# Middle stage of a one-layer streaming encoder: all four engines in program order, attention units as chains, probabilities scaled on VectorE

## The chip, the cores and the metric

One core of one Trainium2 chip runs the kernel. The metric is device microseconds (us) of one execution. TensorE (PE), VectorE (DVE), ScalarE (ACT), GpSimd (POOL) and SyncE (SP, which here issues all DMAs) each take their own instructions in the order of their own queue and wait on semaphores for each other.

## The reference, cut to what matters

```python
def residual_block(x, c, mixer, ...):                 # 512 prompt tokens and 64 sample tokens, D_MODEL = 1024
    sh1, sc1, g1, sh2, sc2, g2 = split(silu(c) @ w_ada + b_ada, 6)
    h = rms_norm(x, norm1_g) * (1 + sc1) + sh1
    mix = mixer(h)                                    # 512 attention columns | 512 convolution columns
    x = x + g1 * (mix @ w_out)
    h = rms_norm(x, norm2_g) * (1 + sc2) + sh2
    return x + g2 * (square(relu(h @ w_ff1)) @ w_ff2)

def mixer(h):
    q, k, v, qi, ki, wi, ga, gb = split(h @ w_in)     # 8 heads x 64; 8 indexer heads x 64
    u = ga * sigmoid(gb)
    sc = einsum(relu(qi . ki / 8), wi * 8 ** -0.5)    # indexer score of every key
    idx = top_k(where(admissible, sc, NEG_INF), k)    # k = 128 (prompt) or 256 (sample, 1088 keys)
    p = softmax(q . k[idx] / 8 - slope * |pos - idx|)
    y = silu(layer_norm(causal depthwise conv(u, 31 taps)))
    return concat(p @ v[idx], y)
```

## The kernel before, in words

Every wide product is an fp32 product in three passes (`mm3`, L288: high by high, high by low, low by high), with tokens along the free dimension in two halves of 288. There are three stages: a start (norm, modulation, first three products), the middle (L488 to L1178), and the second half of the output projection with the MLP. In the start and in the MLP the order of PE, ACT, DVE (in the MLP also POOL) is the order of the program text; in the middle only PE's is (`tc.manual_schedule`, L1153). There a scheduler at compile time orders ACT, DVE and POOL by its own model; `tc.issue_after` ties a few of their instructions to a place.

PE's order in the middle is made by ticks. The main line is 22 column tiles of 128 (`mtile`, L357: 4 `qi`, then three pairs `gb`, `ga`, then `v`, `k`, `q` for four head pairs p), 16 `mm3` each, and then the half of the output projection that reads the convolution (`out_half(mixC)`, L1176), 64 `mm3`. After each `mm3` comes `tick()` (L344). It advances Python generators in the list `side`; each yields the number of ticks to its next step, and what it emits then stands in PE's queue between two `mm3`. `until(cond)` (L353) ticks without any `mm3` between: such ticks take no PE time of their own, and the side steps in them follow each other directly. There are four such loops: in `qkv(0)` until two convolutions are done (L845), in `qkv(p)` for p = 2, 3 until the attention of head pair p - 2 is done, at L1173 until the convolution's norm is done, and at L1177 until no side generator is left.

The side generators: `keys` (indexer keys), `scores` (indexer scores), `topk_prompt` (128 of up to 512 keys, by rounds of max and match-replace on DVE), `topk_sample` (a search over thresholds in 16 iterations: DVE sets candidates, L745, ACT counts with three Sign passes, L747, DVE decides, L748 to L751), `convs` (31 DVE taps for each of channel tiles 0 and 3), `convs_pe` (channel tiles 1 and 2 on PE, L510), `conv_norm`, `attn_prompt` (for each head pair 8 units of logits, softmax, transposition, values), `attn_sample`, `tokens` (k and v written out), `mod_rest` (16 steps of the adaptive modulation; each loads 1 MB of `w_ada` into the two buffers that its predecessor's matmuls have read) and `residual_in`. `P` (L38) holds their waits in ticks; the change leaves `P` as it is.

PSUM banks have four tags: `acc` 3, `lg` 2, `tp` 2, `av` 1. SBUF tags that matter: `pr` 2 (probabilities), `pT` 4 (their transposes; three of them hold the scores at first). A weight tile is split on ACT (`whi`, L331) and POOL (`wlo`, L332) at the start of the column tile before the one that uses it.

Of the kernel before, what the change touches and what calls it, by code (L numbers as in the profile page):

```python
# [71 lines left out]
def step_kernel(ctx: ExitStack, tc: tile.TileContext, io):  # L72
# [153 lines left out]

    def mod_steps(g, f0, nf, operand):
# [21 lines left out]
        if g != 1:  # L249
            o = mod[:, SC1 if g == 0 else SC2, :, r]  # L250
            dve.scalar_tensor_tensor(o, o, 1.0, both((R_G1 if g == 0 else R_G2) + f0), op0=OP.add, op1=OP.mult)

# [90 lines left out]

    def tick():  # L344
# [23 lines left out]
    def evac_stack(dst, scale):  # L368
        def go(j, p, cs_):
            copy_to(act, dst[A, 0, cs_], p[A], scale)  # L370
            copy_to(act, dst[B, 1, cs_], p[B], scale)
            for o, s, hi in ((dst[B, 0, cs_], A, dst[A, 0, cs_]), (dst[A, 1, cs_], B, dst[B, 1, cs_])):
                if scale is None:
                    sub(dve, o, p[s], f(hi))
                else:
                    dve.scalar_tensor_tensor(o, p[s], scale, f(hi), op0=OP.mult, op1=OP.subtract)
# [19 lines left out]
    def front(b):  # L396
        f0, nf = BLOCKS[b]
        g = mod_steps(0, f0, nf, lambda v, kh, kk: ada[b][2 * v + kh][:, kk, :])
        next(g)
        yield  # L400
        pump(g, 1)
# [83 lines left out]
    start.close()  # L485

# [9 lines left out]
    def conv_pe(c):  # L496
# [13 lines left out]
        for h in range(3):  # L510
            t = p_av()
# [5 lines left out]
            act.activation(yc[c][:, CT * h:CT * h + CT], t[:, :CT], AF.Identity, bias=cols[:, R_CB + c:R_CB + c + 1])  # L517
            yield 2
# [22 lines left out]
    def conv_state(c):  # L541
        t = p_tp()
        for s, o in enumerate((SEQ, SEQ + HALO + SAMP)):
            pe.transpose(t[:HALO, 128 * s:128 * s + 128], u[c][:, o:o + HALO], ident)
        m = mt([128, 2, 128], FT, "cso")
        copy_to(act, m[:HALO], t[:HALO, :256].rearrange("p (s x) -> p s x", s=2))
# [34 lines left out]
    def keys():  # L581
        t = p_tp()
        for i in range(5):
            n = 128 if i < 4 else SAMP
            pe.transpose(t[:n, 72 * i:72 * i + 72], kiw[:72, 128 * i:128 * i + n], ident[:72, :72])
        copy_to(act, kiwt[:, :4, :], t[:, :288].rearrange("p (i c) -> p i c", c=72))
# [7 lines left out]
        yield P["KYW"]  # L594
        for b in range(2):
            t = p_tp()
# [5 lines left out]
            yield P["KYW"]  # L602
# [9 lines left out]
    def scores():  # L612
        qis = dt_([128, 4, 2, SAMP], FR, "qis")
# [3 lines left out]
        def prompt(h):  # L617
            for i in (1, 2, 3):
                n = NKEY[i]
                t = p_lg()  # L620
# [3 lines left out]
                r = mt([128, 512], FT, "relu")  # L624
                act.activation(r[:, :n], t[:, :n], AF.Relu)
                if h == 0:
                    dve.tensor_scalar(score[i], r[:, :n], wsc[:, i, 0:1], None, op0=OP.mult)
                else:
                    dve.scalar_tensor_tensor(score[i], r[:, :n], wsc[:, i, h:h + 1], score[i], op0=OP.mult, op1=OP.add)
                if h == 7:  # L630
                    pool.memset(score[i][0:64, n - 64:n], NEG)
                yield P["IDX"]

        def sample(p):
            r = dt_([128, KEYS], FT, "srelu")
            lhs = qis[:, p].rearrange("p s t -> p (s t)")
            for c, (a, b) in enumerate(CH):
                t = p_lg() if c < 2 else p_tp()
# [3 lines left out]
                act.activation(r[:, a:b], t[:, :b - a], AF.Relu)  # L642
                yield P["IDX"] if c < 2 else 1
            if p == 0:
                dve.tensor_scalar(sacc, r, wss[:, 0:1], None, op0=OP.mult)
            else:
                dve.scalar_tensor_tensor(sacc, r, wss[:, p:p + 1], sacc, op0=OP.mult, op1=OP.add)

        def total():
            for a, b, bank_ in ((0, 512, p_lg), (512, KH, p_tp)):  # L650
                t = bank_()
# [3 lines left out]
                copy_to(act, sful[0][:, a:b], t[:, :b - a])  # L655
                yield 2
            spawn(topk_sample(sful[0]), 1)

        for p in range(4):
# [3 lines left out]
            if p < 3:  # L663
                yield from prompt(2 * p)
            yield from sample(p)
# [8 lines left out]
    def distance(i):  # L674
        n = NKEY[i]
        d = mdp.tile([128, 512], FT, name="dist", tag="pr", bufs=2)[:, :n]
        with tc.issue_after(behind[0]):
            pool.iota(d, pattern=[[-1, n]], base=128 * i, channel_multiplier=1, allow_small_or_imprecise_dtypes=True)
        act.activation(d, d, AF.Abs)
        return d  # L680

    last = [None]

    def topk_prompt():
        def steps(*ts):
# [3 lines left out]
            for m, i in zip(m8, ts):  # L689
                last[0] = dve.match_replace(score[i], m, score[i], SENT).ins  # L690

        def penalty(i):
            n = NKEY[i]
            pen = mt([128, 512], FT, "pen")
            dve.tensor_scalar(pen[:, :n], score[i], SENT, BIG, op0=OP.not_equal, op1=OP.mult)
            last[0] = dve.tensor_tensor(dm[i], pen[:, :n], distance(i), op=OP.add).ins
            flags.add(("dm", i))

        for i in (1, 2):
# [5 lines left out]
            penalty(i)  # L705
            yield
        penalty(3)
# [7 lines left out]
    def topk_sample(sful):  # L715
# [28 lines left out]
        for i in range(len(low)):  # L744
            dve.tensor_tensor(sgi[:, 12:15], sgi[:, 8:9].to_broadcast([128, 3]), bits[:, i], op=OP.bitwise_or)  # L745
            for z in range(3):
                act.activation(eq, sful, AF.Sign, bias=cands[:, z:z + 1], scale=-1.0, accum_out=cnts[:, z:z + 1])  # L747
            swap(oths, cnts)  # L748
# [3 lines left out]
            yield P["TKS"]  # L752
# [19 lines left out]
        dve.tensor_scalar(sful, eq, 0.0, BIG, op0=OP.is_equal, op1=OP.mult)  # L772
        act.activation(cum, cum, AF.Abs)
        dve.tensor_tensor(sful, sful, cum, op=OP.add)
        for s, r in enumerate((A, B)):
# [12 lines left out]
    def qkv(p):  # L788
# [4 lines left out]
        def evac_q(j, t, cs_):  # L793
            n = HALF if j == 0 else SEQ - HALF
            r = slice(HALF * j, HALF * j + n)
            for s, (own, oth) in enumerate(((A, B), (B, A))):
                copy_to(act, qd[s][own, 0, r], t[own, :n], 0.125)
                copy_to(act, qd[s][oth, 0, r], t[own, :n], 0.125)
# [612 lines left out]
```

## Time and profile before

| | |
|---|---|
| median of 3 runs | 861.04 us (860.79 to 861.17) |
| profiled execution: time, span | 860.36 us, 858.6 us |
| busy share of the span | PE 94%, DVE 52%, ACT 48%, POOL 35% |
| mean granted TensorE clock | 0.973 |
| the middle | from about 58 to 405 us of the span |

The profile's times are us from the start of the span. A PE that waits inside a run of pipelined matmuls still counts as busy, so the idle time that the view of waits names is the surer figure. A granted clock of 1.0 is 2.4 GHz; the other level is 1.2 GHz.

### The profile page before, as it was taken

How to read it: one execution, taken by the hardware profiler on the slowest of the kernel's cores; microseconds unless marked ns; L12 is line 12 of the kernel's file. 1: busy time of each engine (PE TensorE's matmuls, PEld its weight loads, DVE VectorE, ACT ScalarE, POOL GpSimd, SP SyncE). 2: the span in 40 equal slices, each digit the busy share in tenths (PEclk: the TensorE clock that was granted, in tenths of full speed). 3: DMA queues.
4: the chain of work that ended last, by engine and by line, in shares of the span. 5: the costliest groups of instructions: out<-in, count | busy, mean ns of one | idle time of the engine just before them, and what ended most of it. 6: DMA issues, size and time to landing. Idle time of an engine off the chain costs nothing.

```text
span 858.6 us, 17186 instructions
## 1 busy us (share of the span) xinstructions
PE 808.2 (94%) x6787; PEld 753.0 (88%) x6787; DVE 449.0 (52%) x1148; ACT 412.5 (48%) x976; POOL 303.5 (35%) x337
## 2 busy tenths in 40 slices
PE   5998997989798999999999999999999999999995
PEld 3797895567777988989999999999999999999995
DVE  4569879999997444654934311343113321144142
ACT  5365554555776787754745411443224522244332
POOL 0146342222244414232424343343433343343800
PEclk8799999899999999999999999999999999999998
DMA  8984157247343343732222323223222323223312
GB/s 241 309 205 123 53 146 184 60 100 187 112 113 110 116 137 115 222 122 77 74 74 75 97 76 93 80 75 99 74 77 82 88 83 90 74 74 101 120 55 57
DMA packets 164555, 95.57 MB, mean 111 GB/s; under 512 B 7699, under 2 KB 161119, under 8 KB 164475
## 3 DMA queue, kind: packets, MB, share of 16 engines
q1 hardware_dynamic: 164475, 94.48, 39.2%
q8 instruction: 53, 0.87, 0.4%
q14 instruction: 27, 0.22, 0.1%
HBM read 88.82 MB, written 5.64 MB: 110 GB/s over the span
## 4 chain that ended last, share of the span: by engine, by line
PE 69%; DVE 17%; ACT 7%; DMA 3%; issue 3%; POOL 1%; SPq 0%; ACTq 0%; DVEq 0%; POOLq 0%
PE ps_acc L290 11%; PE ps_acc L291 11%; PE ps_acc L292 11%; PE ps_lg L292 5%; PE ps_lg L290 5%; PE ps_lg L291 5%; DVE yc L564 3%; PE ps_av L292 3%; PE ps_av L290 2%; PE ps_av L291 2%; DVE score L690 2%; DVE m L688 2%; PE ps_tp L234 2%; DMA ada<-w_ada 1%; PE ps_av L887 1%
## 5 line engine op out<-in xcount | busy, mean ns | idle before, releaser
L332 POOL TENSOR_TENSOR wlo<-wraw,whi 128x512 fp32r<-128x512 f32 x172 | 222.6, 1314 | 378.3 <-ACT whi L106 378.0
L290 PE MATMUL ps_acc<-h,whi 128*128 128x288 f32 (+1 forms) x608 | 190.8, 314 | 0.0
L291 PE MATMUL ps_acc<-h,whi 128*128 128x288 f32 (+1 forms) x608 | 181.7, 299 | 0.0
L292 PE MATMUL ps_acc<-h,wlo 128*128 128x288 f32 (+1 forms) x608 | 181.1, 298 | 0.0
L106 ACT ACTIVATE whi<-wraw 128x512 fp32r<-128x512 f32 x172 | 99.8, 621 | 126.4 <-issue 120.6
L290 PEld LDWEIGHTS ps_acc<-h,whi 128*128 128x128 f32 x608 | 116.2, 191 | 14.3 <-issue 12.4
L291 PEld LDWEIGHTS ps_acc<-h,whi 128*128 128x128 f32 x608 | 116.7, 192 | 0.8
L292 PEld LDWEIGHTS ps_acc<-h,wlo 128*128 128x128 f32 x608 | 116.3, 191 | 0.0
L1266 ACT ACTIVATE z<-z,bs 128x224 f32<-128x224 f32 (+2 forms) x96 | 40.2, 450 | 98.6 <-DVE z L1262 98.6
L1087 DVE SCALAR_TENSOR_TENSOR x<-ps_acc,mod,x 128x288 f32<-128x288 f32 (+3 forms) x91 | 36.2, 420 | 83.6 <-PE ps_acc L292 83.0
L564 DVE SCALAR_TENSOR_TENSOR yc<-u,cw,yc 128x606 f32<-128x606 f32 x60 | 58.4, 981 | 0.6
L292 PE MATMUL ps_acc<-a,wlo 128*128 128x288 f32 x192 | 56.7, 295 | 0.0
L290 PE MATMUL ps_acc<-a,whi 128*128 128x288 f32 x192 | 56.6, 295 | 0.0
L291 PE MATMUL ps_acc<-a,whi 128*128 128x288 f32 x192 | 56.6, 295 | 0.0
L292 PE MATMUL ps_lg<-h,wlo 128*128 128x288 f32 (+1 forms) x176 | 52.2, 296 | 0.8 <-POOL wlo L332 0.8
L291 PE MATMUL ps_lg<-h,whi 128*128 128x288 f32 (+1 forms) x176 | 52.2, 297 | 0.0
L290 PE MATMUL ps_lg<-h,whi 128*128 128x288 f32 (+1 forms) x176 | 52.2, 296 | 0.1
L747 ACT ACTIVATE gc<-sful,sg 128x544 bf16<-128x544 f32 x48 | 35.8, 746 | 28.6 <-DVE sg L745 27.8
L872 POOL TENSOR_SCALAR prob<-prob,mx 128x128 f32<-128x128 f32 (+3 forms) x32 | 20.2, 631 | 56.8 <-DVE mx L871 34.2
L1087 DVE SCALAR_TENSOR_TENSOR x<-ps_lg,mod,x 128x64 f32<-128x64 f32 (+4 forms) x34 | 12.7, 407 | 52.5 <-PE ps_lg L292 52.5
L292 PE MATMUL ps_lg<-a,wlo 128*128 128x288 f32 x128 | 37.8, 295 | 0.0
L290 PE MATMUL ps_lg<-a,whi 128*128 128x288 f32 x128 | 37.8, 295 | 0.0
(358 smaller groups left out, 2019.0 us busy)
## 6 DMA issues: line engine op xcount, KB each, us to landing
wraw<-w_ff SPq DMA_DIRECT2D x64, 512.0 KB
ada<-w_ada SPq DMA_DIRECT2D x44, 512.0 KB
wraw<-w_in SPq DMA_DIRECT2D x24, 512.0 KB
wraw<-w_out SPq DMA_DIRECT2D x8, 512.0 KB
rep<-ud SPq DMA_DIRECT2D x24, 115.0 KB
xtok<-x_prompt SPq DMA_DIRECT2D x4, 512.0 KB
ada<-w_ada SPq DMA_DIRECT2D x8, 256.0 KB
ct<-cache_k SPq DMA_DIRECT2D x8, 256.0 KB
```

The costliest lines, as they stand in the source:

```text
L106: act.activation(out, in_, AF.Copy, scale=1.0 if scale is None else scale)
L234: pe.matmul(t[r:r + 32, :w], lhsT=cs[:, 4 * kh + kk, :], rhs=operand(v, kh, kk), start=kk == 0, stop=kk == 3, tile_position=(0, r))
L290: pe.matmul(out, lhsT=hi, rhs=src[:, 0, cs_], start=first, stop=False)
L291: pe.matmul(out, lhsT=hi, rhs=src[:, 1, cs_], start=False, stop=False)
L292: pe.matmul(out, lhsT=lo, rhs=src[:, 0, cs_], start=False, stop=last)
L332: behind[0] = pool.tensor_tensor(lo[:, c], raw[:, c], f(hi[:, c]), op=OP.subtract).ins
L564: dve.scalar_tensor_tensor(yc[c], src, w, yc[c], op0=OP.mult, op1=OP.add)
L688: dve.max(m, score[i])
L747: act.activation(eq, sful, AF.Sign, bias=cands[:, z:z + 1], scale=-1.0, accum_out=cnts[:, z:z + 1])
L872: pool.tensor_scalar(pt[:, :n], pt[:, :n], m[:, 1:2], 1.0, op0=OP.mult, op1=OP.mult)
L1087: dve.scalar_tensor_tensor(xm[:, a:b], t[:, a - r.start:b - r.start], mod[:, g, s, m:m + 1], xm[:, a:b], op0=OP.mult, op1=OP.add)
L1266: act.activation(y, y, AF.Relu, bias=bs[:, s:s + 1])
```

## The change: what it does

It sets ACT, DVE and POOL of the middle in program order too, drops `issue_after`, and moves each step that reads another engine's result some ticks behind it: `after(n, do)` puts a closure into the list `due`, which `tick()` runs n ticks later, before the side generators. A dictionary `room` counts free buffers by tag; `yield from have(tag)` ticks until one is free, `free(tag)` returns it.

What the cut diff below leaves out: in `conv_pe`, `out` is the same activation and then `free(tag)`; in `prompt`, the relu stays in its PSUM bank and `add` frees the bank and does the same multiply-add from there (the third tile uses the `av` bank); `penalty(i)` becomes iota on POOL, 4 ticks, Abs on ACT, 3 ticks, and two DVE steps that reuse the score tile; in `evac_q` and `evac_k` all ACT copies come first, the DVE steps `after(3)` and the copies of their results `after(6)`; a unit of the attention goes on with transpositions, 2 ticks, ACT's copy, 3 ticks, and with s = 1 the values, 2 ticks, ACT, 2 ticks, DVE; `attn_sample` gets such passages too; `spread` gets 2, 2, 2 and 3 ticks between its steps; `conv_norm` uses one `lg` and one `tp` bank for the mean, waits 3 ticks in each of its four steps, 10 in place of CN2, and 2 before each of its four Silu; the last `until` waits for `side` and `due`.

```diff
+    room = dict(tp=2, lg=2, av=1, pr=2, pT=4)
+    def have(tag):
+        while not room[tag]:
+            yield
+        room[tag] -= 1
     def mod_steps(g, f0, nf, operand):
+        yield from have("tp")
         t = p_tp()
         ...
+        yield 3
         copy_to(act, m[:, :w], t[:, :w])
+        free("tp")
         yield P["MODL"]
+        yield from have("tp")
         t = p_tp()
         ...
+        yield 2
     def tick():
+        for e in list(due):
+            e[0] -= 1
+            if e[0] <= 0:
+                due.remove(e)
+                e[1]()
+    inner.enter_context(tc.manual_schedule(engines={mybir.EngineType.PE, mybir.EngineType.Activation, mybir.EngineType.DVE, mybir.EngineType.Pool}))
     def conv_pe(c):
         for h in range(3):
-            t = p_av()
+            tag = ("av", "lg", "av")[h]
+            yield from have(tag)
             ...
-            act.activation(yc[c][:, CT * h:CT * h + CT], t[:, :CT], AF.Identity, bias=cols[:, R_CB + c:R_CB + c + 1])
-            yield 2
+            after(2, out)
+            yield 3
     def scores():
         def prompt(h):
-                r = mt([128, 512], FT, "relu")
-                act.activation(r[:, :n], t[:, :n], AF.Relu)
+                after(2, lambda r=r: act.activation(r, r, AF.Relu))
+                after(4, add)
-            spawn(topk_sample(sful[0]), 1)
+            spawn(topk_sample(sful[0]), 5)
             if p < 3:
                 yield from prompt(2 * p)
+            else:
+                yield 4
             yield from sample(p)
             if p == 3:
                 yield from prompt(2 * p)
+                yield 6
                 yield from total()
-        spawn(topk_prompt(), 1)
+        spawn(topk_prompt(), 6)
     def topk_prompt():
-            penalty(i)
-            yield
-        penalty(3)
+            yield from penalty(i)
+        yield from penalty(3)
     def topk_sample(sful):
             dve.tensor_tensor(sgi[:, 12:15], sgi[:, 8:9].to_broadcast([128, 3]), bits[:, i], op=OP.bitwise_or)
+            yield 3
             ...
+            yield 8
             ...
-            yield P["TKS"]
     def qkv(p):
-        spawn(tokens(1), P["TKW"])
         until(lambda: all(("conv", c) in flags for c in PEC) and (p < 2 or p - 2 in flags))
+        spawn(tokens(1), 4)
-        flags.add(("qkv", p))
+        after(8, lambda: flags.add(("qkv", p)))
     def attn_prompt(p):
+        def unit(i, s):
+            yield from have("lg")
             ...
+            yield 2
+            dve.tensor_reduce(m[:, 0:1], t[:, :n], axis=AX.X, op=OP.max, negate=True)
+            yield 2
+            yield from have("pr")
+            free("lg")
+            act.activation(pt[:, :n], t[:, :n], AF.Exp, bias=m[:, 0:1], accum_out=m[:, 1:2])
+            yield 3
             dve.reciprocal(m[:, 1:2], m[:, 1:2])
-            pool.tensor_scalar(pt[:, :n], pt[:, :n], m[:, 1:2], 1.0, op0=OP.mult, op1=OP.mult)
+            dve.tensor_scalar(pt[:, :n], pt[:, :n], m[:, 1:2], None, op0=OP.mult)
+            yield 2
             ...
+        while left[0] < 4:
+            yield
         flags.add(p)
     def attn_sample(p):
+        yield from logits(1)
+        yield 2
+        yield from logits(2)
+        yield 4
         dve.tensor_reduce(m[:, 3:4], m[:, :3], axis=AX.X, op=OP.max, negate=True)
+        yield 2
         act.activation(pt, pt, AF.Exp, bias=m[:, 3:4], accum_out=m[:, 4:5])
+        yield 4
         dve.reciprocal(m[:, 4:5], m[:, 4:5])
-        pool.tensor_scalar(pt, pt, m[:, 4:5], 1.0, op0=OP.mult, op1=OP.mult)
+        dve.tensor_scalar(pt, pt, m[:, 4:5], None, op0=OP.mult)
         ...
```

## Rows read from the trace of the kernel before

**Rows 1.** Windows: us, then busy us (instructions) of five engines, granted clock, DMA.
```profile
58.00:123.00 65.00, 60.01 (x467) 55.38 (x469) 55.86 (x92) 34.83 (x82) 34.14 (x94) 0.97 0.44 116
123.00:196.00 73.00, 63.58 (x673) 45.77 (x669) 71.14 (x223) 37.07 (x92) 18.67 (x20) 0.94 0.48 124
196.00:257.00 61.00, 52.57 (x505) 46.12 (x498) 57.05 (x123) 41.94 (x114) 19.90 (x17) 0.93 0.51 134
257.00:271.00 14.00, 13.22 (x131) 12.27 (x129) 12.19 (x37) 8.38 (x22) 5.63 (x6) 1.00 0.44 120
271.00:405.00 134.00, 129.82 (x1221) 115.73 (x1219) 65.20 (x185) 90.34 (x232) 44.18 (x50) 0.99 0.44 132
```

**Rows 2.** Waits of PE, 58 to 405 us: total us, times, longest.
```profile
PE ps_av L514 <- ACT yc L517: 6.7, 3, 4.8
PE ps_tp L824 <- ACT kv L106: 4.1, 1, 4.1
PE ps_lg L622 <- ACT relu L625: 3.3, 2, 1.7
PE ps_tp L878 <- POOL prob L872: 3.2, 2, 2.0
PE ps_tp L241 <- ACT modrow L106: 2.3, 1, 2.3
```

**Rows 3.** Timeline of ACT, 147 to 151 us: start, us, instruction, idle before.
```profile
147.51 0.75 ACT L747 ACTIVATE gc<-sful,sg 128x544 bf16<-128x544 f32 x1 [4.00 <-DVE sg L745]
...
150.01 0.41 ACT L517 ACTIVATE yc<-ps_av,cols 128x202 f32<-128x202 f32 x1
```

**Rows 4.** Timeline of DVE: the sum of the convolutions' tiles.
```profile
255.54 0.79 DVE L1023 TENSOR_TENSOR csum<-csum,yc 128x606 f32<-128x606 f32 x1
```

**Rows 5.** Groups of DVE, 58 to 405 us: count, busy us, mean ns, idle before.
```profile
L695 DVE TENSOR_SCALAR pen<-score 128x256 f32<-128x256 f32 (+2 forms) x3 | 1.1, 354 | 0.0
L645 DVE TENSOR_SCALAR sacc<-srelu,wss 128x1088 f32<-128x1088 f32 x1 | 0.8, 787 | 0.0
```

**Rows 6.** Timeline of PE, two ticks apart, without and with a convolution's group.
```profile
131.28 0.30 PE L290 MATMUL ps_acc<-h,whi 128*128 128x288 f32 x1
...
131.67 0.30 PE L290 MATMUL ps_acc<-h,whi 128*128 128x288 f32 x1
...
141.37 0.55 PE L514 MATMUL ps_av<-rep,wd 128*32 128x202 f32 x8
...
142.44 0.55 PE L514 MATMUL ps_av<-rep,wd 128*32 128x202 f32 x8
```

**Rows 7.** Timeline of ACT: copies after `v` of pair 2 and in `q` of pair 2.
```profile
273.54 0.41 ACT L106 ACTIVATE kv<-ps_acc 128x288 f32<-128x288 f32 x1
...
298.50 0.40 ACT L106 ACTIVATE qd<-ps_acc 64x288 fp32r<-64x288 f32 x1
```

**Rows 8.** Waits of DVE, 58 to 405 us.
```profile
DVE mx L871 <- ACT prob L870: 12.7, 19, 1.6
```

**Rows 9.** Timeline of PE: first and last pieces of the end of the middle.
```profile
380.70 0.60 PE L924 MATMUL ps_tp<-ident,ct 128*128 128x128 f32 x4
...
401.69 1.08 PE L234 MATMUL ps_tp<-ada,cs 128*32 128x128 f32 x32
...
404.74 0.39 PE L241 MATMUL ps_tp<-sel,modrow 128*128 128x4 f32 x2
```

**Rows 10.** Chain of work that ended last: start, us, a load of 512 KB.
```profile
56.74 3.46 DMA wraw<-w_in
```

**Rows 11.** Timeline of ACT: table loads in the convolution's norm and after it.
```profile
299.34 1.28 ACT L1003 ACT_TABLE_LOAD   x1
...
312.26 1.28 ACT L1042 ACT_TABLE_LOAD   x1
...
318.34 1.28 ACT L870 ACT_TABLE_LOAD   x1 [0.71 <-DVE mod L248]
```

More of the change, by code (lines that the diff above doesn't have):

```diff
@@ L371, in go, with rest @@
             copy_to(act, dst[B, 1, cs_], p[B], scale)
[L372 to L376, printed above, removed]
+            def rest():
+                for o, s, hi in ((dst[B, 0, cs_], A, dst[A, 0, cs_]), (dst[A, 1, cs_], B, dst[B, 1, cs_])):
+                    if scale is None:
+                        sub(dve, o, p[s], f(hi))
+                    else:
+                        dve.scalar_tensor_tensor(o, p[s], scale, f(hi), op0=OP.mult, op1=OP.subtract)
+            after(2, rest)
         return go
@@ L541, in conv_state @@
     def conv_state(c):
+        yield from have("tp")
         t = p_tp()
@@ L581, in keys @@
     def keys():
+        yield from have("tp")
         t = p_tp()
@@ L617, in prompt @@
         def prompt(h):
+            while "wi" not in flags:
+                yield
             for i in (1, 2, 3):
                 n = NKEY[i]
-                t = p_lg()
+                tag = ("lg", "lg", "av")[i - 1]
+                yield from have(tag)
+                t = (p_lg, p_lg, p_av)[i - 1]()
                 lhs = qi[h // 2][:, h % 2, 128 * i:128 * i + 128]
@@ L637, in sample @@
             for c, (a, b) in enumerate(CH):
+                tag = "lg" if c < 2 else "tp"
+                yield from have(tag)
                 t = p_lg() if c < 2 else p_tp()
@@ L894, in attn_prompt @@
-        for x in range(len(units) + 3):
-            if 0 <= x - 2 < len(units):
-                turn(x - 2)
-            if x < len(units):
-                while units[x][0] and ("dm", units[x][0]) not in flags:
-                    yield
-                logits(x)
-            if x >= 4 and x % 2 == 0:
-                values((x - 4) // 2)
-            yield P["ATT"]
+            free("pr")
+            yield 2
+            yield from have("pT")
+            free("tp")
+            probT[i, s] = mdp.tile([128, 512], FT, name="probT", tag="pT", bufs=4)
@@ new lines, in unit @@
+            copy_to(act, probT[i, s][:, :n], t[:, :n])
+            yield 3
+            if s:
+                while (i, 0) not in probT:
+                    yield
+                yield from have("av")
+                av = p_av()
+                pts = [probT.pop((i, z)) for z in range(2)]
+                for c in range(i + 1):
+                    for z in range(2):
+                        pe.matmul(av[64 * z:64 * z + 64, :128], lhsT=vt[:, c, 64 * z:64 * z + 64],
+                                  rhs=pts[z][:, 128 * c:128 * c + 128], start=c == 0, stop=c == i, tile_position=(0, 64 * z),
+                                  skip_group_check=True)
+                r = slice(128 * i, 128 * i + 128)
+                free("pT", "pT")
+                yield 2
+                copy_to(act, mixT[p][:, 0, r], av[:, :128])
+                yield 2
+                sub(dve, mixT[p][:, 1, r], av[:, :128], f(mixT[p][:, 0, r]))
+                free("av")
+                left[0] += 1
@@ L904, in attn_prompt @@
+        for i in range(4):
+            for s in range(2):
+                while i and ("dm", i) not in flags:
+                    yield
+                spawn(unit(i, s))
+                yield P["ATT"]
+        while left[0] < 4:
+            yield
         flags.add(p)
@@ L1010, in spread @@
         pe.matmul(tb[:, :SAMP], lhsT=ones, rhs=dg[:, SEQ:TOK], start=True, stop=True)
+        yield 2
+        free("tp", "tp")
         copy_to(act, dst[:, :SEQ], ta)
         copy_to(act, dst[:, S], tb[:, :SAMP])
-        yield
+        yield 3
     mixC = []
     def conv_norm():
-        while "taps" not in flags:
+        while not ("taps" in flags and all(("conv", c) in flags for c in PEC)):
             yield
@@ L1147, in convs @@
             for _ in range(W - P["T0"] if c == 0 else W):
-                with tc.issue_after(last[0]):
-                    next(taps[c])
+                next(taps[c])
                 yield P["TAP"]
         flags.add("taps")
-    with tc.manual_schedule(engines={mybir.EngineType.PE}):
-        spawn(prepare(), P["PRW"])
-        spawn(keys(), P["KEYW"])
-        spawn(convs(), P["TAPW"])
-        spawn(convs_pe(), 8)
-        spawn(scores(), P["SCW"])
-        spawn(mod_rest(), P["MODW"])
-        for p in range(4):
-            mtile(evac_stack(qi[p], None))
-            spawn(bump(), P["QIW"])
-            if p == 0:
-                spawn(conv_state(0), P["CS0"])
-        glu(1)
-        glu(2)
-        glu(3)
-        spawn(conv_norm(), P["CNW"])
-        spawn(chain(*[attn_prompt(p) for p in range(4)]))
-        spawn(samples())
-        for p in range(4):
-            qkv(p)
-        until(lambda: "norm" in flags)
-        mix_conv()
-        spawn(residual_in())
-        out_half(mixC, lambda m, j: None)
-        until(lambda: not side)
+    spawn(prepare(), P["PRW"])
+    spawn(keys(), P["KEYW"])
+    spawn(convs(), P["TAPW"])
+    spawn(convs_pe(), 8)
+    spawn(scores(), P["SCW"])
+    spawn(mod_rest(), P["MODW"])
+    for p in range(4):
+        mtile(evac_stack(qi[p], None))
+        spawn(bump(), P["QIW"])
+        if p == 0:
+            spawn(conv_state(0), P["CS0"])
+    glu(1)
+    glu(2)
+    glu(3)
+    spawn(conv_norm(), P["CNW"])
+    spawn(chain(*[attn_prompt(p) for p in range(4)]))
+    spawn(samples())
+    for p in range(4):
+        qkv(p)
+    until(lambda: "norm" in flags)
+    mix_conv()
+    spawn(residual_in())
+    out_half(mixC, lambda m, j: None)
+    until(lambda: not side and not due)
+    inner.close()
     mid.close()
```

247 lines of the change are left out of this document (163 added, 84 removed).

## The prediction

> **What bounds the kernel now.** I read the windows first, to see which engine is full in which stretch; then the waits of PE, to see who holds it up; then the timelines around the longest waits. From 123 to 257 us DVE is busy 128.2 of 134 us, and PE idles 17.9 us there; from 271 to 405 us PE is busy 129.8 of 134 us and DVE half of it [rows 1]. So the middle has two parts: one in which DVE is full and PE waits now and then, and one in which PE alone is full. Over the whole middle PE idles 27.8 us (the windows' lengths less PE's busy times), and the granted clock is 0.93 to 0.97 in the first three windows: 65 x 0.03 + 73 x 0.06 + 61 x 0.07 + 134 x 0.01 = 12 us of full-clock time that was not granted [rows 1]. In such gaps the clock falls to the lower of its two levels. More than 12 + 27.8 us cannot be had.
>
> The waits are of one kind. Twelve lines make 27.2 us; the five shown make 19.6, and ACT ends 16.4 of these, POOL 3.2 [rows 2]. ACT is not full (31% idle at least in each window). It is held by order: its three Sign passes stand at the head of its queue and wait 4.00 us for DVE's candidates, and the copy that frees the convolution's bank stands behind them and starts at 150.01 [rows 3]; PE's longest wait, 4.8 us [rows 2], ends with it.
>
> **What program order does to the first part.** The change puts every step of the other engines where the program has it, so an evacuation stands behind the DVE work of earlier ticks and not behind that of later ones. The waits of [rows 2] go where DVE keeps up. But DVE's work does not shrink, so I ask how far PE is when DVE ends the convolution's taps; after that PE alone bounds.
>
> Ticks, counted from the first tile of the middle by the code. Before: `scores` ends at 94, rounds of top-k from 95, 16 rounds of 112 ticks and two single ticks, "prompt" at 209, 84 ticks of taps, "taps" at 293. After: four ticks and six ticks more make `scores` end at 104; the spawn waits 6 (110); 112 ticks of rounds; three penalties of 7; "prompt" at 243; "taps" at 327. In `qkv(0)` the loop without main work ran from 176 to 202; the two convolutions of PE now end near 217 (ten ticks for `scores`, one more per bank), so it runs 41 ticks and not 26. Main ticks behind "taps": 267 before, 286 after.
>
> DVE before ended that sum at 255.54 + 0.79 = 256.3 us [rows 4]. After, it starts the rounds some 2 us later, and has by tick 327 this work besides: the end of the sample's selection and pair 1's `q`, which before lay in 257 to 271 us (12.2 us busy [rows 1], of which I take 10), and the scaling of pair 0's probabilities: 8 of 0.354 us [rows 5] = 2.8. So DVE is there at 256.3 + 2 + 12.8 = 271 us. The 24 other scalings of units and the 4 of 0.787 us [rows 5] (11.6 us) fall behind 271 us, where DVE idles 68.8 of 134 us [rows 1]; they cost nothing while that holds.
>
> PE leads DVE, but no more than about one column tile: a weight's `whi` stands in ACT's queue behind copies that wait for DVE, and the tile after next needs it. I take 12 ticks. So at 271 us PE has 286 + 12 = 298 main ticks done. Before, at 273.54 us it had just ended `v` of pair 2 [rows 7], which is main tick 272 (298 less the 26 without main work). That is 26 main ticks ahead: at 131.67 - 131.28 = 0.39 us [rows 6], 10.3 us. Side work is ahead too: from 273.54 to 298.50 us (`q` of pair 2, 24 main ticks on [rows 7]) the PE took 25.0 us, 9.4 of it main ticks; of the 15.6 of side work and stalls I count half, 7.8, as done by then in the new order, since the attention of pair 1 starts 28 ticks later than before and sample 0 ten. Bounds 0 and 15.6. Gain: 18.1 us.
>
> **What it adds there.** DVE now stops where its next instruction is not ready. The nearest row: DVE's reciprocal waits for ACT's exponentials 12.7 us in 19 times, 0.67 each [rows 8]. Between ticks 110 and 327 there are some 12 iterations of the sample search, 8 units and 4 evacuations of such passages: 24 x 0.67 = 16 us at most, 0 where DVE is late anyway. DVE is the late engine there, so I take a quarter, 4 us.
>
> The convolutions' 48 groups of PE cost 1.07 us with their tick [rows 6], 0.68 over a plain one, in either order. In the longer loop of `qkv(0)` 24 groups lie alone, which DVE's rounds cover: it is full there. Without that cover the loop's 15 more ticks would cost PE 15 x 0.39 = 6 us.
>
> **The end of the middle.** Before, the last `w_ada` step came at 401.69 and the last product of the side work at 404.74 us [rows 9]: main line (tick 442), samples (450) and modulation (446 for step 16) ended together. After, a modulation step takes 27 + 5 = 32 ticks, so step 16 is at 41 + 15 x 32 = 521; a sample takes some 52 ticks in place of 40, from about 301, so the last ends near 509; the main line ends at 352 + 41 + 5 + 64 = 462 (5 for the loop of pair 3, as pair 1 ends near 366). From 462 on there is no `mm3` between the pieces: the last sample's chain, 457 to 509, is bare. Before it ran from 380.70 to 404.74, 24 us [rows 9] with 30 main ticks of 0.39 beside it, so 12 us of other work and passages. Behind it comes step 16, whose loads can start only when step 15 has read its buffers; a load of 512 KB took 3.46 us [rows 10], two take 4 to 7. I take 18 us for this end, in which PE has some 10 us of work of its own (that sample, the last units of pair 3, two steps). Cost: 8 us. Bounds: 0, if waits for buffers make the main line later and so cover it, and 24 - 10 = 14.
>
> What else moves: SP's queue has the same DMAs, two loads each per modulation step later; POOL loses 32 + 4 scalings and so frees itself for `wlo`, which nobody waited long for. After 271 us I set new waits equal to the 4.2 us that go. The sum: -18.1 + 4 + 8 = -6.1; 860.4 - 6.1 = 854.3, and the median of the runs lies 0.7 above the profiled execution: 855.
>
> **Rivals.**
>
> 1. DVE in order falls behind, and ACT with it (slower). Place: ticks 110 to 327. Price: the full 16 us of bare passages, 12 more than counted, and PE loses the lead of 12 ticks (4.7): 855 + 17 = 872. For: DVE is at 97% there, ACT's longest single cause of waiting is DVE [rows 3]. Against: a late engine seldom waits. It decides from a sum L1023 that ends after 281 us; forecast 275, this rival 288.
> 2. DVE does not bind PE: evacuations stand early enough, and all waits on ACT and POOL go (19.3 + 4.6 us of the twelve lines) with their share of the clock (10.5): 860.4 - 34.4 + 8 + 0.7 = 835. Against: DVE's 128 us of work in 134 [rows 1].
> 3. No change: ACT loads a function table in 1.28 us each time, three times in the norm before, because its Sqrt and four Silu fell between the exponentials of two head pairs [rows 11]. After, the norm comes at ticks 336 to 391 and pair 2's exponentials from 378 on, one every 4 ticks, while the Silu stand 2 ticks apart: some 8 loads, 5 more, 6.4 us on ACT. If PE waits for each: 855 + 6.4 = 861.5. Against: ACT idles 43.7 of 134 us there [rows 1].
>
> The Trainium skill, "ScalarE: Activation LUTs", section "Table sets: the hidden batching unit", says to batch calls by table set and not by function, which speaks against this interleaving; its section "What ACT_TABLE_LOAD costs" gives 1283 ns and 1380 ns of drain. The trace agrees on the load, 1.28 us [rows 11]; the drain is not to be seen in these rows. By the page's sum rival 3 would end at 855 + 5 x 2.66 = 868.
>
> **Numbers.** A difference under 0.2% (859.3 to 862.8) cannot be told from none. Forecast 855, own range 848 to 859: 0.38. Rival 2: 0.12. Rival 3: 0.15. Rival 1: 0.35. Faster 0.50, same 0.15, slower 0.35. The unknown terms span -25.9 (front with all side work, no end) to +19.7 (front 10.3, 16 and 14); a range of 841 to 877 leaves out most of rival 2 and the far end of rival 1.
>
> **What would show it.** Right: PE's waits for ACT `yc` L517 and `kv` L106 and for POOL's probabilities gone; L1023's successor ends near 275 us; PE mostly idle or sparse for some 8 us ahead of the products on `mix`; ACT table loads 8 or so in the norm. Wrong: that sum beyond 281 us, PE waits in the first part that end with `wlo` or with DVE, the last sample covered by main work, or a part of the time moving outside 58 to 405 us.

## The result, and the profile after

912.32 us median (909.70 to 913.18, 4 runs) against 861.11 (860.79 to 861.65, 4 runs): ratio 1.0589 [1.0565, 1.0613], slower by 51.2 us. The forecast was 855, range 841 to 877. The profiled execution has a span of 911.1 us at a mean granted clock of 0.948 (before 858.6 and 0.973).

Windows of the kernel after, the edges and columns of [rows 1] (TensorE's matmuls, its weight loads, VectorE, ScalarE, GpSimd):

```profile
58.00:123.00 65.00, 62.25 (x482) 57.71 (x481) 53.64 (x85) 35.58 (x82) 35.28 (x92) 1.00 0.46 122
123.00:196.00 73.00, 66.70 (x776) 50.73 (x775) 62.62 (x208) 35.92 (x89) 14.75 (x16) 0.95 0.56 139
196.00:257.00 61.00, 39.05 (x281) 35.81 (x279) 52.70 (x131) 37.59 (x99) 15.28 (x12) 0.83 0.34 93
257.00:271.00 14.00, 11.13 (x92) 9.98 (x92) 13.56 (x30) 8.69 (x21) 2.45 (x4) 0.76 0.07 19
271.00:405.00 134.00, 115.11 (x921) 101.38 (x915) 72.59 (x174) 82.27 (x199) 27.88 (x20) 0.87 0.36 105
```

Up to 196 us PE is busier than before. From 196 on it idles 22 of 61 us and the clock is at 0.83, and no other engine is full for long: DVE idles 8.3 of these 61 us and ACT 23.4. That is the sign of engines that wait for each other.

One window over the middle up to the same product, the 17th `mm3` on `mix` (411.4 us before, 463.0 after); first before, then after:

```profile
58.00:411.40 353.40, 325.60 (x3024) 281.68 (x3023) 266.93 (x676) 217.04 (x554) 125.10 (x188) 0.97 0.45 125
```

```profile
58.00:463.00 405.00, 346.31 (x3026) 301.46 (x3025) 286.59 (x713) 224.72 (x559) 103.31 (x150) 0.91 0.40 110
```

The window is 51.6 us longer: PE's idle time goes from 27.8 to 58.7 us (30.9 more), and its busy time from 325.6 to 346.3 (20.7 more) for the same matmuls, since more of them run at the clock's lower level (granted clock 0.97 before, 0.91 after). Of 5 us lost, 2 are clock.

Where it goes, by the start of the first `mm3` behind k main ticks in PE's timelines (TensorE's side work between them differs, so this is the lead of the main line alone). Before in us, the others as difference to it, a minus for ahead; e1 to e17 are experiments below:

| main tick | before | after | e3 | e1 | e14 | e17 |
|---|---|---|---|---|---|---|
| 144 | 167.5 | -17.2 | -18.8 | -6.5 | -8.6 | -16.4 |
| 160 (`v` of pair 0) | 177.4 | -13.0 | -14.6 | -2.1 | -4.4 | -12.2 |
| 180 (in `k`, behind the loop of `qkv(0)`) | 204.8 | -11.4 | -7.4 | +16.1 | +10.4 | +7.4 |
| 192 (`q` of pair 0) | 209.8 | -3.8 | -6.3 | +17.2 | +11.7 | +9.3 |
| 208 | 223.7 | -7.6 | -12.2 | +14.3 | +10.6 | +2.7 |
| 256 | 262.2 | +9.4 | +4.7 | +12.5 | +16.0 | +5.3 |
| 304 | 308.1 | +10.5 | -2.3 | +2.7 | +8.4 | -1.3 |
| 368 | 364.4 | +34.8 | +13.4 | +17.2 | +19.6 | +13.3 |
| 416 (first on `mix`) | 405.0 | +32.4 | +10.8 | +14.4 | +17.3 | +10.6 |
| 476 | 428.9 | +52.5 | +31.2 | +33.5 | +17.3 | +30.1 |

After: a lead of 17.2 us at 150 us (main tick 144), 13.0 at main tick 160, 9.2 of it lost by main tick 192, 36.2 us lost from there to main tick 416, 20.1 at the end. The MLP changes nothing: the spans of the two profiled executions differ by 52.5 us, as the starts of main tick 476 do.

Of the 9.2 us, only 1.6 are gone by main tick 180: the loop of `qkv(0)` took 19.7 us and 17.8 before, from one `mm3` around it to the next. Some 7 us go at one place behind it, between main ticks 190 and 191. There ACT's Sign passes wait for DVE, ACT's copy of `kvtok` stands behind them, and PE waits for the copy (ACT, then PE):

```profile
199.02 0.75 ACT L827 ACTIVATE gc<-sful,sg 128x544 bf16<-128x544 f32 x1 [4.02 <-DVE sg L824]
...
202.55 0.57 ACT L106 ACTIVATE kvtok<-ps_tp 128x512 f32<-128x512 f32 x1
```

```profile
203.18 1.93 PE L247 MATMUL ps_tp<-ada,cs 128*32 128x128 f32 x32 [4.87 <-ACT kvtok L106]
```

Waits of TensorE in the kernel after, 58 to 463 us (total us, times, longest); the lines that answer to [rows 2]:

```profile
PE ps_tp L985 <- DVE prob L980: 7.6, 1, 7.6
PE ps_tp L923 <- ACT kv L106: 5.2, 1, 5.2
PE ps_tp L247 <- ACT kvtok L106: 4.9, 1, 4.9
PE ps_tp L247 <- DMA ada<-w_ada: 4.6, 2, 3.6
PE ps_tp L985 <- DVE mod L265: 3.1, 1, 3.1
PE ps_tp L1094 <- DVE sprob L1085: 3.0, 1, 3.0
```

The waits for `yc` and for POOL's probabilities are gone, as forecast; the one for `kv` is longer, and DVE now ends three of six. How the one for `kv` arises is read from three timelines (start, us, instruction, idle before), first DVE:

```profile
226.39 3.51 DVE L607 SCALAR_TENSOR_TENSOR yc<-u,cw,yc 128x606 f32<-128x606 f32 x4
...
230.93 0.16 DVE L824 TENSOR_TENSOR sg<-sg,bits 128x3 int32<-128x3 int32 x1
```

then ACT and PE:

```profile
231.19 0.75 ACT L827 ACTIVATE gc<-sful,sg 128x544 bf16<-128x544 f32 x1 [4.24 <-DVE sg L824]
...
233.68 0.39 ACT L106 ACTIVATE kv<-ps_acc 128x288 f32<-128x288 f32 x1
```

```profile
234.12 0.69 PE L923 MATMUL ps_tp<-ident,kv 128*128 128x128 f32 x2 [5.24 <-ACT kv L106]
```

DVE's candidates stand behind four taps, ACT's Sign passes wait 4.24 us for them, the copy of `kv` stands behind the Sign passes, and PE waits 5.24 us for the copy, with DVE's next max behind PE in turn. The longest wait has one place too: the selection of the sample ends with a block of DVE steps from 248.5 to 258.7 us that the program packs into three ticks, and a unit's max (L972) stands near its end. ACT idles 6.06 us for the max, and PE 7.59 us for the scaling (DVE, ACT, PE):

```profile
256.99 0.55 DVE L972 TENSOR_REDUCE mx<-ps_lg 128x1 f32<-128x384 f32 x1
257.46 0.77 DVE L849 SCALAR_TENSOR_TENSOR gc<-sful,sg,gc 128x544 bf16<-128x544 f32 x1
258.27 0.44 DVE L852 TENSOR_SCALAR sful<-gc 128x544 f32<-128x544 bf16 x1
...
258.82 0.35 DVE L980 TENSOR_SCALAR prob<-prob,mx 128x256 f32<-128x256 f32 x1
```

```profile
257.57 0.58 ACT L977 ACTIVATE prob<-ps_lg,mx 128x384 f32<-128x384 f32 x1 [6.06 <-DVE mx L972]
```

```profile
259.23 0.69 PE L985 MATMUL ps_tp<-ident,prob 128*128 128x128 f32 x2 [7.59 <-DVE prob L980]
```

### The profile page after: what moved, and what is told of

It is laid out like the page before. It is cut to its first block, busy times and chain, and to the rows that moved or that the text cites. A ratio compares the mean times of both kernels' runs of the same rounds, so it can differ in the third digit from the quotient of the medians.

```text
span 911.1 us, 17105 instructions
## 1 busy us (share of the span) xinstructions
PE 826.0 (91%) x6787; PEld 771.3 (85%) x6787; DVE 469.6 (52%) x1184; ACT 419.4 (46%) x980; POOL 280.4 (31%) x301
## 4 chain that ended last, share of the span: by engine, by line
PE 68%; DVE 10%; ACT 8%; issue 2%; POOL 0%; ACTq 0%; DVEq 0%
PE ps_acc L308 12%; PE ps_acc L309 11%; PE ps_acc L310 11%; PE ps_lg L310 5%; PE ps_lg L309 5%; PE ps_lg L308 5%; PE ps_av L310 2%; PE ps_av L309 2%; PE ps_av L308 2%; DVE yc L607 2%; DVE score L770 2%; DVE m L768 1%; ACT qd L106 1%; PE ps_tp L247 1%; DVE sg L808 1%
## 5 line engine op out<-in xcount | busy, mean ns | idle before, releaser
L350 POOL TENSOR_TENSOR wlo<-wraw,whi 128x512 fp32r<-128x512 f32 x172 | 225.9, 1334 | 535.0 <-ACT whi L106 531.1
L308 PE MATMUL ps_acc<-h,whi 128*128 128x288 f32 (+1 forms) x608 | 195.1, 321 | 2.1 <-DVE qbd L892 1.7
L309 PE MATMUL ps_acc<-h,whi 128*128 128x288 f32 (+1 forms) x608 | 185.1, 304 | 0.0
L310 PE MATMUL ps_acc<-h,wlo 128*128 128x288 f32 (+1 forms) x608 | 184.4, 303 | 0.0
L308 PEld LDWEIGHTS ps_acc<-h,whi 128*128 128x128 f32 x608 | 120.1, 197 | 15.0 <-issue 10.7
L309 PEld LDWEIGHTS ps_acc<-h,whi 128*128 128x128 f32 x608 | 120.4, 198 | 1.0
L310 PEld LDWEIGHTS ps_acc<-h,wlo 128*128 128x128 f32 x608 | 119.6, 197 | 0.0
L1251 DVE SCALAR_TENSOR_TENSOR x<-ps_acc,mod,x 128x64 f32<-128x64 f32 (+3 forms) x91 | 35.5, 419 | 89.2 <-PE ps_acc L310 89.2
L247 PE MATMUL ps_tp<-ada,cs 128*32 128x128 f32 (+1 forms) x672 | 29.7, 312 | 11.8 <-DMA ada<-w_ada 5.8
L1251 DVE SCALAR_TENSOR_TENSOR x<-ps_lg,mod,x 128x64 f32<-128x64 f32 (+4 forms) x34 | 12.7, 406 | 52.5 <-PE ps_lg L310 52.5
```

The costliest lines, as they stand in the source:

```text
L308: pe.matmul(out, lhsT=hi, rhs=src[:, 0, cs_], start=first, stop=False)
L309: pe.matmul(out, lhsT=hi, rhs=src[:, 1, cs_], start=False, stop=False)
L310: pe.matmul(out, lhsT=lo, rhs=src[:, 0, cs_], start=False, stop=last)
L350: behind[0] = pool.tensor_tensor(lo[:, c], raw[:, c], f(hi[:, c]), op=OP.subtract).ins
L1251: dve.scalar_tensor_tensor(xm[:, a:b], t[:, a - r.start:b - r.start], mod[:, g, s, m:m + 1], xm[:, a:b], op0=OP.mult, op1=OP.add)
```

## Experiments

The kernel before took 860.6 to 861.5 us beside these runs. No kernel leaves work out.

**Whose order costs? (e1, e2, e3)** The line that sets program order, with fewer engines (their names are shortened here): e1 PE alone; e2 PE, ACT, POOL; e3 PE, DVE, POOL.

```diff
-    inner.enter_context(tc.manual_schedule(engines={PE, Activation, DVE, Pool}))
+    inner.enter_context(tc.manual_schedule(engines={PE}))
```

> The changed kernel with its new steps and its new order of TensorE, but ACT, DVE and POOL of the middle ordered at compile time again. Theory A (DVE and ACT in program order hold PE up between 216 and 399 us of the changed kernel's span, where it loses 42 us to the kernel before): most of that comes back, 865 to 885 us; the bare end of some 22 us stays. Rival B (the new order of TensorE itself, with its deferred steps and its waits for buffers, makes the gaps): 900 to 915, the same PE waits at the transpositions.

> The changed kernel, with DVE alone ordered at compile time; PE, ACT and POOL stay in program order. If the DVE's order is the place (serial steps of the sample's selection and the taps stand ahead of an attention unit's max and scaling): 875 to 890, near the run with all three free. If it is ACT's (Sign passes at the head of its queue): 905 to 915. By rival B: 905 to 915 too, and the run with all three free tells that apart.

> The changed kernel, with ACT alone ordered at compile time; PE, DVE and POOL stay in program order. If the Sign passes that wait for DVE at the head of ACT's queue are the place: 880 to 895 and no wait of PE for kv or kvtok over 3 us. If it is DVE's order: 905 to 915.

Measured: e1 895.12 (892.89 to 898.62), e2 913.09, e3 891.37; ratios 1.0399 [1.0369, 1.0428], 1.0604 [1.0588, 1.0620], 1.0348 [1.0331, 1.0365]. ACT's order costs 21 us, and DVE's by itself nothing. e1 lies between the ranges of its two theories, so neither holds alone. DVE's columns (third pair) from 123 us to the sum of the convolutions' tiles, before, after, in e2 and in e1:

```profile
123.00:255.54 132.54, 114.69 (x1158) 90.44 (x1151) 126.77 (x340) 77.59 (x202) 37.30 (x37) 0.94 0.49 126
```

```profile
123.00:301.43 178.43, 142.58 (x1312) 119.79 (x1311) 152.07 (x405) 96.03 (x246) 40.04 (x37) 0.88 0.41 107
```

```profile
123.00:294.90 171.90, 139.41 (x1319) 116.92 (x1317) 131.34 (x392) 95.22 (x241) 40.41 (x40) 0.90 0.42 110
```

```profile
123.00:236.95 113.95, 92.34 (x944) 71.40 (x942) 110.48 (x311) 55.17 (x138) 23.61 (x25) 0.88 0.46 115
```

DVE idles 5.8 us before, 26.4 after, 40.6 in e2, 3.5 in e1. My reading is that a DVE that may choose has nothing to choose from while ACT's queue, in order, feeds it. Up to the 17th `mm3` on `mix`, e3 is 21.8 us shorter than after, and only 5.2 of that is idle time of PE (58.7 to 53.5); 16.6 is busy time (346.3 to 329.7 for the same matmuls), the clock's part (0.91 to 0.95).

**The end (e4, e7).** e4 is `MOD=21` to 16 alone; e7 that and

```diff
-            yield 8
+            yield 5
             swap(oths, cnts)
```

> The changed kernel with P[MOD] 16 in place of 21: a modulation step takes 27 ticks again and not 32, so the sixteenth comes some 75 ticks earlier, inside the main line. Theory A with its bare end: the two pieces of modulation behind the last sample (454.8 to 460.8 us) go from there, 5 to 8 us gained, 904 to 907. Rival (the last sample's chain alone sets the end, or the earlier steps only crowd the middle): within 2 us of 912.

> The changed kernel, all four in program order; the search waits 5 ticks and not 8 after its Sign passes (48 ticks less over 16 iterations) and P[MOD] is 16, so that samples and modulation end with the main line, near tick 475 and not 526 and 558. Theory T (the end of the middle costs 20 us in every run so far because the samples outlast the main line; MOD alone could not change it): 890 to 897. Rival (DVE and ACT, more crowded before tick 260, lose as much as the end gives back): 907 to 917.

Measured: e4 913.53 (1.0610 [1.0594, 1.0625]), no change; e7 897.48 (1.0427 [1.0409, 1.0446]), 14.8 less, a hair outside what was expected. The last sample sets the end and not modulation, as the rival of e4 had it. In the kernel after, the last sample's scaling ends PE's wait at 450.24 us, 13 us behind the first product on `mix` (437.37).

**What in ACT's and DVE's order? (e5, e6, e8)** e5: `yield 3` to 6 ahead of the Sign passes and 8 to 5 behind them. e6: four multiplications, `yield 2`, then the four Silu. e8, which also shortens the search:

```diff
-            yield 8
+            yield 6
             swap(oths, cnts)
...
+        yield 4
         count(up, OP.is_ge)
+        yield 4
...
-        yield
+        yield 4
         dve.tensor_tensor_scan(cum, eq, eq, 0.0, op0=OP.add, op1=OP.bypass)
```

> The changed kernel, all four engines in program order; in the search of the sample's selection the three Sign passes come 6 ticks behind DVE's candidates and not 3, and DVE's decision 5 ticks behind them and not 8. Theory A1 (what ACT in order costs, 21.7 us by the run with ACT free, is the Sign passes that wait for DVE at the head of ACT's queue): 892 to 903. Rival A2 (ACT is held by all its passages alike, exponentials and copies that stand two ticks behind DVE or PE): 908 to 914.

> The changed kernel, all four in program order; the four Silu of the convolution's norm stand together behind the four multiplications, not 2 ticks apart between exponentials. The function table is loaded 8 times in the norm of the changed kernel (1.28 us each); this leaves 3 or 4. If the loads delay PE one for one: 6 us less, 905 to 908. If ACT has room for them: 910 to 914.

> The changed kernel, all four in program order; the serial section that ends the sample's selection (some 25 DVE steps, 8.4 us, packed into 3 ticks) is spread over 28 ticks, and the search waits 6 ticks and not 8 so that the sample's flag comes 7 ticks earlier and not later. If the DVE block at 248 to 259 us is a main place of the loss (PE waits 7.6 us behind it, and the clock falls): 898 to 905. If it is only one of many: 907 to 912.

Measured: e5 904.08 (1.0507 [1.0491, 1.0523]), between the two theories: Sign passes at the head of ACT's queue are worth 8 of the 21 us. e6 910.58 (1.0583 [1.0567, 1.0599]), not to be told from 912.3, though 4 of the 8 table loads are gone from the norm. e8 901.75 (1.0487 [1.0465, 1.0509]), 10.6 less. Its edit has two parts, and they were not run apart: in its timeline 7.0 us are gained by main tick 416 (+25.4), and 3.9 more behind it, where the samples come earlier. So the block of DVE steps is worth some 7 us, if the shorter search gained nothing before the end.

**Together (e9, e10).** e9: e6, e8 and `MOD=16`, with the Sign passes 5 ticks behind the candidates and the decision 4 behind them, the sums ahead of `prompt(6)`, samples 7 ticks shorter; e10 the same with ACT free.

> The changed kernel, all four in program order, with the four edits together: Sign passes 5 ticks behind the candidates (decision 4 ticks later), Silu grouped, the serial section spread, MOD 16; and to bring the last sample to the end of the main line, the sums before two prompt scores and 7 ticks less for each sample. If the losses lie in different places they add up: 8 + 2 + 15 + 10 = 35 us, 877. If they are one and the same lag of DVE and ACT, seen in several places: 888 to 897.

> The kernel of the four edits together, with ACT alone ordered at compile time. The end is mended here too (15 to 20 us of 891.4). If ACT's order and the edits of the search price the same stall: 870 to 877. If the serial section's 10 us come on top: 860 to 868, level with the kernel before. Above 885: the mended end gives its gain back in the middle.

Measured: e9 903.20 (1.0495 [1.0473, 1.0516]), worse than both expectations and no better than e8 alone; e10 892.22 (1.0365 [1.0340, 1.0389]). The end is gone in both (first on `mix` +41.6 and main tick 476 +41.5 in e9, +32.6 and +32.5 in e10), but at the first on `mix` e9 is 9 us later than after, and e10 22 us later than e3: what the end gave is lost in the middle, as the last expectation of e10 had it. With every queue in order, a mended place moves the wait to the next one, for instance

```profile
PE ps_lg L973 <- ACT prob L982: 15.8, 4, 9.4
```

in e9, where the kernel after had 2.2 us on that pair.

**One part of the change alone (e11, e12, e13).** e11: the kernel before with four engines in order and without `issue_after`. e12: the kernel after with the scaling on POOL. e13: the kernel before with

```diff
-            pool.tensor_scalar(pt[:, :n], pt[:, :n], m[:, 1:2], 1.0, op0=OP.mult, op1=OP.mult)
+            dve.tensor_scalar(pt[:, :n], pt[:, :n], m[:, 1:2], None, op0=OP.mult)
```

> The kernel before with one part of the change alone: all four engines of the middle in program order, the three ties to a place dropped, no deferred steps. If the ticks between the engines are what makes program order bearable: over 930, PE waits at most evacuations. If program order by itself costs what ACT's costs in the changed kernel (21.7 us): 880 to 890.

> The changed kernel with one part undone: the probabilities are scaled on POOL again. DVE has 14.4 us less work, 2.8 of it before its taps end. If DVE's load in program order sets the lag: 903 to 908. If the move cost nothing, as the forecast had it (its price hidden in DVE's idle time): 909 to 914. If POOL's slower passage shows: 914 to 922.

> The kernel before with one part of the change alone: probabilities scaled on DVE, not POOL; ACT, DVE and POOL ordered at compile time as before. In the changed kernel undoing this part cost 7.4 us. If the scaling on DVE is a gain by itself (POOL ends 3.2 us of PE's waits before): 854 to 859. If its gain there came from the program order alone: 860 to 863. If DVE's load matters: over 863.

Measured: e11 951.32 (1.1060 [1.1032, 1.1089]); program order costs 90 us there, and the kernel after, which has the deferred steps and the other parts too, is 39 faster. e12 919.67 (1.0691 [1.0669, 1.0712]): undoing the scaling costs 7.4 us in program order, where PE comes two ticks behind it:

```profile
PE ps_tp L985 <- POOL prob L980: 12.2, 5, 7.6
```

e13 864.19 (1.0040 [1.0028, 1.0052]): alone in the kernel before, the same edit loses 3.5 us, which fits the expectation that DVE's load matters there; the cause was not tested further.

**Two causes or one? (e14, e15, e16)** e14: e1 with e7's edits. e15: e9's edits with PE alone in order. e16: `T0=20` to 31.

> The changed kernel with ACT, DVE and POOL ordered at compile time (895 us) and the early end (search 5 ticks after its Sign passes, MOD 16). Theory C (the loss has two independent parts: ACT and DVE starving each other in program order, and the end, where samples outlast the main line): 872 to 880. Rival D (the end's gain is given back in the middle, as in the run with the four edits together): 888 to 896.

> The kernel of the four edits together with ACT, DVE and POOL ordered at compile time. Theory C: 868 to 878, the sum over the convolutions' tiles ends before 245 us and DVE idles under 8 us from 123 us until then. Rival D: 888 to 896.

> The changed kernel, all four in program order, with the whole first channel tile's taps (31, not 20) ahead of the sample's and prompt's selections, in a stretch where DVE idles more, and 11 of the 43 taps (9.6 us of DVE) taken out of ticks 246 to 329. Theory E (from tick 246 on PE goes at DVE's pace): the sum ends 8 to 12 us earlier and the time is 898 to 905. Rival (waits between engines, not DVE's work, set the pace): 908 to 914.

Measured: e14 877.98 (1.0206 [1.0191, 1.0222]); e15 881.36 (1.0243 [1.0228, 1.0258]), 3 above the range; e16 910.55 (1.0585 [1.0563, 1.0606]), so the rival holds there. Order and end are separate and add up within 2.3 us:

| | end as changed | early end | difference |
|---|---|---|---|
| four engines in order | 912.3 | 897.5 | 14.8 |
| PE alone in order | 895.1 | 878.0 | 17.1 |
| difference | 17.2 | 19.5 | |

The remaining 17.3 us of e14 over before lie for the most part in the loop of `qkv(0)` (from -4.4 at main tick 160 to +10.4 at 180). There no `mm3` stands between the side steps, and the compiled order has put nine Sign passes, each three behind a DVE step, ahead of the copy that the next modulation matmul needs. Its wait in PE's timeline of e14:

```profile
208.41 0.38 PE L257 MATMUL ps_tp<-sel,modrow 128*128 128x4 f32 x1 [14.25 <-ACT modrow L106]
```

The kernel after has no such wait (PE waits 0.9 us in all for `modrow` at that line) and loses 1.6 us from main tick 160 to 180, where e14 loses 14.8. So this place tells where e14 is slow, and not where the kernel after is.

In e16 the sum ends at 287.7 us, 14.5 earlier than after, and the time does not move: PE does not go at the pace of DVE's taps.

**Program order for the first part only (e17, e18).** At the end of the loop in `qkv(0)`:

```diff
+        if p == 0:
+            inner.close()
+            inner.enter_context(tc.manual_schedule(engines={PE}))
```

e18 adds `MOD=16`, 6 and 5 ticks ahead of and behind the Sign passes until the switch and then 3 and 3, and samples 7 ticks shorter.

> The changed kernel, all four engines in program order only until the two convolutions on PE are done (main tick 176); from there ACT, DVE and POOL are ordered at compile time. Theory C: program order is a gain ahead of that place (the changed kernel leads by 12 us at main tick 176, by 8 at 208) and the starving lies behind it, so the lead is kept to the end of the main line and only the end's 20 us are left: 868 to 878. If the lag is built up ahead of that place and only shows behind it: 888 to 900.

> The same, with Sign passes 6 ticks behind the candidates (decision 5 later) until the switch, a search of 6 ticks per iteration after it, MOD 16, and samples 7 ticks shorter, so that samples and modulation end with the main line. Theory C: the lead of 12 us at main tick 208 stays, the last sample's 7 to 10 us of work move into the main line, no end: 852 to 860, a little faster than the kernel before. Rival D (what is gained at the end is given back in the middle): 865 to 878.

Measured: e17 890.73 (1.0352 [1.0323, 1.0382]), e18 893.43 (1.0380 [1.0358, 1.0402]): both miss theory C; e17 lies in its second range, with the lag built up ahead of the switch, and e18 in neither of its two. The table above shows what held in e17: from main tick 192 to 416 it loses 1.3 us and not 36.2. What failed is the lead: 19.6 us went from main tick 160 to 180, in the loop, where the kernel after loses 1.6. So a part of the later loss only moved forward: from main tick 160 to 416 e17 loses 22.8 us and the kernel after 45.4. About half of that loss is thus owed to order behind the loop, and the 21 us of e3 agree. The longest waits in e17 and in e18 are

```profile
PE ps_tp L247 <- DMA ada<-w_ada: 11.6, 2, 10.5
```

```profile
PE ps_lg L1068 <- POOL dms L108: 15.5, 1, 15.5
```

The first lies in the loop; in the second the samples come before POOL has copied the selection. No version tried is as fast as the kernel before.

## Why the prediction was wrong

The ticks, counted in the program, were nearly right: `scores` 105 (forecast 104), "prompt" 244 (243), "taps" 329 (327), main end 470 (462), samples 526 (509), last modulation step 537 (521). By 271 us PE was to have 298 main ticks done; it had 255 (before: 272). What was built on the ticks failed at two steps of the same kind. One is **"a late engine seldom waits"**, with its 4 us for waits in the first part: at main tick 256 the kernel is 9.4 us behind, where the sum had it 14.1 ahead, 23.5 us in all. The other is **"after that PE alone bounds"**, with its term "After 271 us I set new waits equal to the 4.2 us that go": from there to main tick 416 another 23.0 us go, forecast 0. The end was under-sized by 12.1. In both steps the waits of engines on each other in order were left out.

- *The front, -18.1.* A lead of that size was there, by luck, since it came at another place and not from the terms of the sum: 17.2 us at main tick 144, 150 us. (26 ticks of 0.39 us are 10.1, not 10.3.) It did not last to 271 us. The loop of `qkv(0)`, whose bare ticks I had priced at 6 us and then hidden behind DVE, took only 1.9 more than before; the rest went behind it, first to the wait for `kvtok`.
- *Where DVE is at the end of the taps, 275 us.* 302.2, against 256.3 before [rows 4]. In the windows from 123 us DVE's busy time is 25.3 us longer (forecast 12.8), and its idle time 20.6 us longer, where I took a quarter of 16 since "a late engine seldom waits". My reading is that it does wait when the engine that feeds it waits for it in turn: in the rows above ACT waits for DVE, PE for ACT, and DVE's next max stands behind PE.
- *Rival 1* had the sign and the place, and its mark (a sum beyond 281 us) came true; ACT was held by DVE, as it says. But DVE's lateness as the cause did not hold: with DVE's order free (e2) the time stays, in e16 the sum ends earlier and in e1 at 237.7 us, 18.6 earlier than before, and the times are 910.6 and 895.1. The late sum was a symptom.
- *After 271 us, 0.* From main tick 256 to 416 the lag grows from 9.4 to 32.4 us. I reasoned that DVE idles half of that part and PE alone is full [rows 1], so nothing could be held up. An engine with idle time still holds up another when its next instruction in order is not ready. In e17, where ACT and DVE may choose, it grows by 5.3.
- *The end, +8, bounds 0 to 14.* The direction was right and the size too small: 20.1 us in the timeline, 14.8 to 17.1 by e7 and e14. Products on `mix` stand between the last steps in PE's timeline, so it is not bare, but they too wait.
- *Scaling on DVE, nothing.* It is worth 7.4 us with the rest of the change (e12) and costs 3.5 without it (e13).
- *Rival 3, table loads.* Eight from the norm on, as forecast (three before [rows 11]); the first two and the last (ACT's timeline):

```profile
339.57 1.28 ACT L1152 ACT_TABLE_LOAD   x1
348.71 1.28 ACT L977 ACT_TABLE_LOAD   x1
...
365.16 1.28 ACT L977 ACT_TABLE_LOAD   x1
```

  With four of them gone (e6) the time moved by 1.7 us, within the intervals. ACT's spare time did hide them, as far as these four show.
- *What every term lacked:* the clock. I counted a wait of 1 us as 1 us, except in rival 2. The middle lost 30.9 us of idle time and 20.7 us of busy time to the clock.

By e1, e7 and e14, of the 51.2 us some 15 to 17 are the end, 17 to 20 program order of ACT with DVE, and 17 are what e14 leaves, where PE alone keeps its new order. The first two are shown by the runs. The third is not located in the kernel after, since in e14 it lies for the most part in a wait that the kernel after does not have; its cause stays open. How the clock's part splits over the three was not measured by itself.

## What to carry to other kernels

Program order on several engines at once made a ring of queues here, and the slack of each engine is worth nothing where its next instruction waits for another of the ring; ask of each instruction that waits what stands behind it and who waits for that, engine by engine, until you are back at the first. Try to free the engine that feeds the others (here ACT, 21 us) before the full one (here DVE, nothing), and price a gap of PE with the clock that it costs. Effects that were each worth 8 to 15 us by themselves did not add up where they sat in the same ring; those with separate causes (order, end) did, within 2.3 us.

## What the runs showed of the hardware

- The granted clock fell with the scattered gaps: 0.73 in this window of the kernel after, in which PE did 12.43 us of work in 20, and 1.00 again where it ran nearly without gaps, 432.50 us of work in 434.

```profile
236.00:256.00 20.00, 12.43 (x67) 11.37 (x65) 18.35 (x50) 9.82 (x30) 4.37 (x4) 0.73 0.22 59
466.00:900.00 434.00, 432.50 (x3243) 430.66 (x3243) 149.47 (x390) 160.65 (x350) 167.83 (x133) 1.00 0.28 81
```

  Products of one shape start 0.13 us apart at the upper of the two levels and 0.24 at the lower, both seen within 1.4 us, just behind a gap of 2.37 us (PE after):

```profile
460.75 0.40 PE L308 MATMUL ps_acc<-mix,whi 128*128 128x288 f32 x1 [2.37 <-DVE x L1251]
...
461.26 0.29 PE L308 MATMUL ps_acc<-mix,whi 128*128 128x288 f32 x1
461.39 0.29 PE L309 MATMUL ps_acc<-mix,whi 128*128 128x288 f32 x1
...
462.34 0.45 PE L308 MATMUL ps_acc<-mix,whi 128*128 128x288 f32 x1
462.58 0.45 PE L309 MATMUL ps_acc<-mix,whi 128*128 128x288 f32 x1
```

  So here part of a gap's price came after it.
- A change of function table took 1.28 us and no more in these rows: ACT's copy ends at 351.10, the load runs from 351.12, and the Silu starts at 352.41.

```profile
350.84 0.26 ACT L106 ACTIVATE vsn<-ps_tp 64x128 f32<-64x128 f32 x1
351.12 1.28 ACT L1203 ACT_TABLE_LOAD   x1
352.41 0.87 ACT L1203 ACTIVATE yc<-yc,cols 128x576 f32<-128x576 f32 x1
```

  The Trainium skill, "ScalarE: Activation LUTs", section "What ACT_TABLE_LOAD costs", adds 1380 ns of drain to 1283 ns of load. The load agrees; the drain does not show in these rows, where the whole passage is 1.31 us, and the measurement decides.
